# Row chunks behind all products of an input job, and the convolution tile behind the chunks

## The chip, the cores and the metric

The kernel runs on one core of one Trainium2 chip. The metric is the time of one execution on the device in microseconds; the median of several runs is given.

## What is computed

One decoder layer on 256 tokens of width 2048, in float32: a norm, a gated projection, a causal depthwise convolution of 31 taps, a layer norm, an output projection, and an MLP. Six vectors, made from a condition `c`, scale and shift it. Cut to what matters:

```python
mod = silu(c) @ mod_w + mod_b
sh1, sc1, g1, sh2, sc2, g2 = split(mod, 6)
h = rms_norm(x, norm1_g) * (1 + sc1) + sh1
a, gt = split(h @ conv_w_in + conv_b_in, 2)
u = depthwise_conv(a * sigmoid(gt), conv_dw_w) + conv_dw_b   # 31 taps, causal
u = silu(layer_norm(u, conv_ln_g, conv_ln_b))
x = x + (1 + g1) * (u @ conv_w_out + conv_b_out)
h = rms_norm(x, norm2_g) * (1 + sc2) + sh2
x = x + (1 + g2) * (square(relu(h @ mlp_w1)) @ mlp_w2)
```

## The kernel before

Activations lie with channels on the 128 partitions and 256 tokens in the free dimension: 16 tiles of 128 channels. Weights come as blocks of 1 MB through the tag `raw` with seven buffers, in one fixed order that `order` lists and `top_up` issues on SyncE's queue; a block is issued when a buffer comes free. Each weight block is split by `split_w` into a rounded part `hi` (ScalarE, L206) and a rest `lo` (L209, on GpSimd for the input jobs), in halves, so that products in a fast format keep float32's precision.

The work is a list of `jobs`: 16 input jobs, 8 output jobs, then the MLP's. Input jobs 0 to 7 are done in the first stage while the columns of `sc1` and `sh1` arrive. Input jobs 8 to 15 stand in the loop shown below, and `n` is their number. Such a job

- makes the gate's two channel tiles: `mm` issues 64 products (L234 and L235; job 15 uses a merged form, L230 to L232) in four quarters, two outputs by two halves of the contraction, into one of two accumulators of the tag `mm` (one accumulator has two PSUM banks);
- runs up to four **row chunks**. `mod_chunk` (L310) multiplies the condition with one block of `mod_w`; the rows for `g1` and `sc2` make 32 chunks: 4 in each of jobs 8 to 12, 3 in job 13, 9 in job 15. A chunk is four matmuls of 32 columns of the array, eight records in the trace. When 16 chunks are done the sums are copied (L317) and turned into columns (L357);
- evacuates its accumulator (`evac`, L518 on ScalarE and L519 on VectorE) and gates it (`gate`, L750 and L752);
- from job 9 on runs one **convolution tile** on TensorE (`mix`, `pe_conv`, L735): 32 matmuls of 32 columns, 64 records, into an accumulator of the same tag `mm`; ScalarE copies it out (L743). The operand is a widened copy of `u` (`copy_wide`, L712, two buffers). Eight more channel tiles are convolved on VectorE, tap by tap (`advance`, L621 to L630). After the second convolution tile, `find_shift` sums two tiles (L410), and ScalarE copies the negative mean (L670), which VectorE adds (L625, L674).

The layer norm's sums over channels are taken by `stats` in groups of four tiles: ScalarE squares them (L462, one buffer `sq`), and TensorE sums tiles and squares (L680). Group 0 and group 1 stand behind job 14's products, group 2 behind the convolution tile of job 15. Then come two row chunks, the last convolution tile (into the tag `acc`), the last sums and the norm itself.

A scheduler fixes each engine's order when the program is built: of what is ready by its own estimate of times it takes the piece written first (pieces in `urgent()` come earlier). `tc.issue_after(ins)` adds one bound: what stands inside is queued behind `ins` on the same engine. It does not wait for `ins` to finish, and it does not keep other work out from between.

Of the kernel before, what the change touches and what calls it, by code (L numbers as in the profile page):

```python
# [66 lines left out]
def conv_block(ctx: ExitStack, tc: tile.TileContext, x, vec, dwq, c_row, mod_r, mod_c, w_first, w_in, w_out, w1, w2, out):  # L67
# [50 lines left out]
    state = {"used": 0}  # L118
# [103 lines left out]
    def mm(p, c, key, acts_of, ks=range(KT), merged=False):  # L222
        halves = parts[key]
        for k in ks:
            hi, lo = halves[k // HALF]
            m = acts_of[k // 2][:, k % 2, :]
            if merged:
                out_p, begin, end = p[:, c, 0:T], k == 0, k == KT - 1
                w = hi[:, k % HALF, :]
                nc.tensor.matmul(out_p, w, m[:, 0:T], start=begin, stop=False)  # L230
                nc.tensor.matmul(out_p, w, m[:, T : 2 * T], start=False, stop=False)  # L231
                state["mm_end"] = nc.tensor.matmul(out_p, lo[:, k % HALF, :], m[:, 0:T], start=False, stop=end)  # L232
                continue
            nc.tensor.matmul(p[:, c, :], hi[:, k % HALF, :], m, start=(k == 0), stop=(k == KT - 1))  # L234
            state["mm_end"] = nc.tensor.matmul(  # L235
                p[:, c, T : 2 * T], lo[:, k % HALF, :], m[:, 0:T], start=False, stop=(k == KT - 1),
                skip_group_check=True,
            )
# [62 lines left out]
    def mod_chunk(nb, kg):  # L301
        w = take(("mod", nb, kg))
        group = next(g for g in GROUPS if nb in g)
        b = group.index(nb)
        begin, end = b == 0 and kg == 0, b == len(group) - 1 and kg == 3
        if begin:
            mod_finish()
            row_ps.append(ps.tile([P, 512], F32, name="row", bufs=1))
        for k in range(4):
            state["row_end"] = nc.tensor.matmul(  # L310
                row_ps[0][32 * k : 32 * k + 32, :], cz[:, 4 * kg + k, 3 - b : 35 - b], w[:, 4 * k : 4 * k + 4, :],
                start=begin, stop=end,
            )
        if end:
            r = tmp.tile([P, 512], F32, name="rowsb", bufs=1)
            with urgent(), tc.issue_after(state["hi_end"]):
                nc.scalar.activation(r, row_ps.pop(), AF.Copy)  # L317
            pending.append(([4 * nb for nb in group], 4, r))

    def shift_row(at, w):  # L320
        if at == 0:
            row_ps.append(ps.tile([P, 512], F32, name="row", bufs=1))
        for k in range(KT):
            g = k % 4
            nc.tensor.matmul(
                row_ps[0][32 * g : 32 * g + 32, at * P : (at + 1) * P], shz[:, k, :], w[:, k, :],
                start=(k < 4), stop=(k >= KT - 4),
            )

    def fold_shift():  # L330
        n = 2 * UNSCALED
        r = tmp.tile([P, 512], F32, name="rowsb", bufs=1)
        p = ps.tile([P, 512], F32, name="row", bufs=1)
        with urgent():
            nc.scalar.activation(r[:, 0 : n * P], row_ps.pop()[:, 0 : n * P], AF.Copy)
            for j in range(n):
                nc.tensor.matmul(p[:, j : j + 1], r[:, j * P : (j + 1) * P], col("pick", 0, 1), start=True, stop=True)
            nc.scalar.activation(shc, p[:, 0:n], AF.Copy)
# [40 lines left out]
    def mod_col(at, w=None):  # L379
        w = (take(("col", at)) if w is None else w).rearrange("p k n -> p (k n)")  # L380
        which, k = divmod(at, KT)
        acc = modc[:, at : at + 1]
        if which == SH2 and "cond" in state:
            n = HALF * P
            for half, total in zip(state["cond"], (acc, rest2[:, k : k + 1])):
                nc.vector.scalar_tensor_tensor(w[:, 0:n], w[:, 0:n], 1.0, half, op0=ALU.mult, op1=ALU.mult, accum_out=total)
                w = w[:, n:]
            return
        with tc.issue_after(state["e_end"]) if "e_end" in state else ExitStack():
            nc.vector.scalar_tensor_tensor(w, w, 1.0, cb, op0=ALU.mult, op1=ALU.mult, accum_out=acc)  # L390
        if which in amps:
            return nc.vector.scalar_tensor_tensor(
                amps[which][:, k : k + 1], acc, col("modb", at), col("n1g", k), op0=ALU.add, op1=ALU.mult
            )
        elif which != SH2:
            return mod_bias(at, 1, acc)

    def mods(keys):
        for key in keys:
            if key[0] == "mod":  # L400
                mod_chunk(*key[1:])
            else:
                mod_col(key[1])
# [28 lines left out]
    def two():  # L432
        return tmp.tile([P, 2, T], F32, name="two", bufs=6)
# [26 lines left out]
    def squares(src, s=None):  # L460
        s = cp.tile([P, 4, T], F32, name="sq", bufs=1) if s is None else s
        nc.scalar.activation(s, src, AF.Square)  # L462
        return s
# [8 lines left out]
    def by_tokens(job):  # L472
        return job[0] == "down" or job[0] == "up" and job[1:] not in ((0, 0), (0, 1))
# [133 lines left out]
    def cv(k):  # L607
        return cvs[k // 4][:, k % 4, :]
# [67 lines left out]
    def sum_round(pairs, first=False, last=()):  # L676
        for n, tiles in enumerate(zip(*pairs)):
            for m, t in enumerate(tiles):
                g = 2 * n + m
                state["stats_end"] = nc.tensor.matmul(  # L680
                    state["small"][32 * g : 32 * g + 32, 0:T], ones[:, 0:32], t, start=first, stop=m in last,
                )

    def stats(b):
        s = squares(cvs[b])
        for k in range(2):
            sum_round([(cv(4 * b + 2 * m + k), s[:, 2 * m + k, :]) for m in range(2)], b == 0 and k == 0)
# [69 lines left out]
    def mix(ct):  # L757
        pe_conv(ct)
        if ct == SHIFT - 1:
            find_shift()  # L760
# [15 lines left out]
    for n, job in enumerate(jobs):  # L776
# [22 lines left out]
        if job == ("up", 0, 0):  # L799
            mm(p, 0, job + (0,), xa, range(SIDE))  # L800
            for at in range(2 * UNSCALED):
                shift_row(at, shown.pop(("up", 0, at // 2, at % 2)))
            fold_shift()
            mm(p, 0, job + (0,), xa, range(SIDE, KT))
            mm(p, 1, job + (1,), xa)
        elif job in K_OUTER:
            for k2 in range(HALF):
                for c in range(2):
                    mm(p, c, job + (c,), xa if plain else hl, range(2 * k2, 2 * k2 + 2), kind == "out")
        elif kind == "in":  # L810
            rows = [key for key in after[job] if key not in cols_in] if i < KT - 1 else []
            for c in range(2) if i < KT - 1 else (1, 0):
                for ks in (range(HALF), range(HALF, KT)):
                    mm(p, c, job + (c,), hl, ks, i == KT - 1)
                    with tc.issue_after(state["mm_end"].ins):
                        mods(rows[:1])
                    del rows[:1]
        elif by_tokens(job):
            mm_tokens(sums[kind, i // 2], job, u2 if kind == "down" else hl, n == len(jobs) - 1)
        else:  # L820
            for c in range(2):
                mm(p, c, job + (c,), hl, merged=kind == "out")
        mod_finish()
        if kind == "in":
# [11 lines left out]
                for key, w in taken:  # L836
                    mod_col(key[1], w)
            for ct in CONV_AT.get(n, ()):
                with tc.issue_after(state["mm_end"].ins):
                    mix(ct)  # L840
            advance(ADVANCE.get(n, 0))
            if n == KT - 2:
                with tc.issue_after(state["mm_end"].ins):
                    for b in range(2):
                        stats(b)
            if n < KT - 1:
                continue
            sq15 = two()
            with tc.issue_after(state["conv_end"].ins):
                stats(2)  # L850
            rows = list(after[job])
            with tc.issue_after(state["stats_end"].ins):
# [226 lines left out]
```

## Time and profile before

| | us |
|---|---|
| median of 3 runs | 1103.8 |
| lowest and highest | 1103.57, 1103.97 |
| the profiled execution | 1103.93 |
| its span, first to last instruction | 1102.1 |

| engine | busy us | share of the span |
|---|---|---|
| TensorE (PE) | 1085.5 | 98% |
| its weight loads (PEld) | 892.8 | 81% |
| VectorE (DVE) | 746.3 | 68% |
| ScalarE (ACT) | 510.2 | 46% |
| GpSimd (POOL) | 192.7 | 17% |

The span is 1.8 us shorter than the time of the execution. L310 and the like are lines of the kernel. "Busy" counts the time in which an engine has an instruction in work; gaps of TensorE between matmuls of different kinds are not seen in it, since matmuls are pipelined and their ends are modelled. A row of the chain gives start, length and what ran, followed back from the last instruction; "x8" counts records.

### The profile page before, as it was taken

What the parts mean: (1) busy time and instruction counts of PE and PEld (TensorE: products, weight loads), DVE (VectorE), ACT (ScalarE), POOL (GpSimd) and SP (SyncE); (2) the same over time, 40 slices, a digit from 0 to 9 for tenths busy, and PEclk for the clock granted to TensorE, in tenths of its full rate; (3) what the DMA queues carried; (4) which work ended last, traced back from release to release, by engine and by line L of the source; (5) the groups of instructions that cost most, each with busy time, mean ns of one, the idle gap of its engine ahead of it and who ended that gap; (6) DMA issues with size and microseconds to landing.
All of it is one profiled execution on the core that took longest, in us unless ns stands there. A gap on an engine that the chain in (4) does not pass through costs nothing.

```text
span 1102.1 us, 15388 instructions
## 1 busy us (share of the span) xinstructions
PE 1085.5 (98%) x6018; PEld 892.8 (81%) x6018; DVE 746.3 (68%) x1025; ACT 510.2 (46%) x679; POOL 192.7 (17%) x119
## 2 busy tenths in 40 slices
PE   7999999999999999999999999999999999999998
PEld 4887876667599998888888888888888888888887
DVE  5777789989676966678954667545566665565653
ACT  4111296665676587444443444333444333444431
POOL 0000076468679252000000000000000000000000
PEclk9999999999999999999999999999999999999999
DMA  9999999876899966898976889657888877789611
GB/s 385 421 420 420 416 408 356 349 288 264 321 359 419 402 240 232 255 317 304 418 285 218 237 267 319 236 141 290 249 234 245 234 210 210 229 247 244 206 67 39
DMA packets 142316, 314.23 MB, mean 285 GB/s; under 512 B 87586, under 2 KB 105506, under 8 KB 107298
## 3 DMA queue, kind: packets, MB, share of 16 engines
q1 hardware_dynamic: 142096, 313.11, 80.8%
q8 instruction: 47, 0.77, 0.3%
q14 instruction: 27, 0.21, 0.1%
q10 hardware_dynamic: 146, 0.13, 0.0%
HBM read 301.15 MB, written 12.07 MB: 284 GB/s over the span
## 4 chain that ended last, share of the span: by engine, by line
PE 88%; DMA 9%; DVE 2%; ACT 1%; issue 0%; SPq 0%; ACTq 0%
PE mm L258 20%; PE mm L257 20%; PE mm L259 20%; DMA raw<-mod_c 9%; PE mm L234 6%; PE mm L235 3%; PE acc L232 2%; PE acc L231 2%; PE acc L230 2%; PE mm L735 2%; PE row L310 2%; DVE raw L390 1%; PE mm L231 1%; DMA x<-x 1%; PE mm L230 1%; PE mm L232 1%
## 5 line engine op out<-in xcount | busy, mean ns | idle before, releaser
L206 ACT ACTIVATE hi<-raw 128x1024 fp32r<-128x1024 f32 x320 | 335.6, 1058 | 367.9 <-PE mm L259 333.6
L209 DVE TENSOR_TENSOR lo<-raw,hi 128x1024 fp32r<-128x1024 f32 x257 | 313.2, 1223 | 193.5 <-ACT hi L206 191.4
L258 PE MATMUL mm<-lo,u 128*128 128x512 f32 x496 | 193.0, 389 | 0.0
L257 PE MATMUL mm<-hi,u 128*128 128x512 f32 x496 | 193.0, 389 | 0.0
L259 PE MATMUL mm<-hi,u 128*128 128x512 f32 x496 | 192.9, 389 | 0.0
L209 POOL TENSOR_TENSOR lo<-raw,hi 128x1024 fp32r<-128x1024 f32 x63 | 154.3, 2476 | 199.1 <-DMA raw<-w_in 132.2
L259 PE MATMUL mm<-hi,hl 128*128 128x512 f32 x480 | 186.7, 389 | 0.0
L258 PE MATMUL mm<-lo,hl 128*128 128x512 f32 x480 | 186.7, 389 | 0.0
L257 PE MATMUL mm<-hi,hl 128*128 128x512 f32 x480 | 186.7, 389 | 0.0
L390 DVE SCALAR_TENSOR_TENSOR raw<-raw,cond 128x2048 f32<-128x2048 f32 x50 | 118.2, 2366 | 39.8 <-DMA raw<-mod_c 39.6
L259 PEld LDWEIGHTS mm<-hi,u 128*128 128x128 f32 x496 | 93.1, 188 | 19.4
L258 PEld LDWEIGHTS mm<-lo,u 128*128 128x128 f32 x496 | 93.1, 188 | 19.0
L257 PEld LDWEIGHTS mm<-hi,u 128*128 128x128 f32 x496 | 93.1, 188 | 19.0
L257 PEld LDWEIGHTS mm<-hi,hl 128*128 128x128 f32 x480 | 90.1, 188 | 18.8
L259 PEld LDWEIGHTS mm<-hi,hl 128*128 128x128 f32 x480 | 90.1, 188 | 18.7
L258 PEld LDWEIGHTS mm<-lo,hl 128*128 128x128 f32 x480 | 90.1, 188 | 18.7
L627 DVE SCALAR_TENSOR_TENSOR acc<-u,v,acc 128x256 f32<-128x256 f32 x224 | 94.4, 483 | 1.8
L234 PE MATMUL mm<-hl,hi 128*128 128x512 f32 x224 | 81.7, 406 | 0.0
L562 PE MATMUL mm<-two,first 128*128 128x256 f32 x256 | 61.1, 394 | 7.6 <-ACT two L593 7.5
L562 PEld LDWEIGHTS mm<-two,first 128*128 128x128 f32 x256 | 49.9, 197 | 17.5 <-ACT two L593 10.4
L232 PE MATMUL acc<-hl,lo 128*128 128x256 f32 x224 | 63.5, 283 | 0.0
L235 PE MATMUL mm<-hl,lo 128*128 128x256 f32 x224 | 63.4, 283 | 0.0
(183 smaller groups left out, 1278.6 us busy)
## 6 DMA issues: line engine op xcount, KB each, us to landing
raw<-w SPq DMA_DIRECT2D x128, 1024.0 KB, 5.4
raw<-mod_c SPq DMA_DIRECT2D x62, 1024.0 KB, 11.4
raw<-mod_r SPq DMA_DIRECT2D x32, 1024.0 KB, 7.8
raw<-w_in SPq DMA_DIRECT2D x16, 1024.0 KB, 8.0
raw<-w_out SPq DMA_DIRECT2D x16, 1024.0 KB, 7.8
first<-w_first SPq DMA_DIRECT2D x15, 1024.0 KB, 19.8
flat<-two SPq DMA_DIRECT2D x30, 256.0 KB, 2.7
two<-flat SPq DMA_DIRECT2D x120, 64.0 KB, 4.1
```

The source lines that it names most:

```text
L206: state["w_hi"] = nc.scalar.activation(hi, w[:, ks, :], AF.Copy).ins
L209: end = by.tensor_tensor(lo, w[:, ks, :], hi.bitcast(F32), op=ALU.subtract)
L230: nc.tensor.matmul(out_p, w, m[:, 0:T], start=begin, stop=False)
L232: state["mm_end"] = nc.tensor.matmul(out_p, lo[:, k % HALF, :], m[:, 0:T], start=False, stop=end)
L234: nc.tensor.matmul(p[:, c, :], hi[:, k % HALF, :], m, start=(k == 0), stop=(k == KT - 1))
L235: state["mm_end"] = nc.tensor.matmul(p[:, c, T : 2 * T], lo[:, k % HALF, :], m[:, 0:T], start=False, stop=(k == KT - 1), skip_group_check= ...
L257: nc.tensor.matmul(p, p_hi, hi, start=begin, stop=False)
L258: nc.tensor.matmul(p, p_hi, lo, start=False, stop=False)
L259: nc.tensor.matmul(p, p_lo, hi, start=False, stop=end)
L390: nc.vector.scalar_tensor_tensor(w, w, 1.0, cb, op0=ALU.mult, op1=ALU.mult, accum_out=acc)
L562: step = nc.tensor.matmul(held[n][:, c, :], w[:, 2 * n + c, :], h, start=k == 0 and c == 0, stop=k == KT - 1, skip_group_check=True)
L627: nc.vector.scalar_tensor_tensor(out, s, w, acc, op0=ALU.mult, op1=ALU.add)
```

## The change

In the input jobs 8 to 14 the chunks are no longer queued one behind each quarter of the products; all of a job's chunks are queued behind the job's last product. The convolution tile is no longer queued behind the last product but behind the last chunk, where the job has chunks. Group 0 of the norm's sums is queued behind the convolution tile of job 14 and not behind its last product. Group 1 moves from job 14 to job 15: it is queued behind that job's convolution tile, ahead of group 2.

```diff
             for c in range(2) if i < KT - 1 else (1, 0):
                 for ks in (range(HALF), range(HALF, KT)):
                     mm(p, c, job + (c,), hl, ks, i == KT - 1)
-                    with tc.issue_after(state["mm_end"].ins):
-                        mods(rows[:1])
-                    del rows[:1]
+            state["step_end"] = state["mm_end"]
+            with tc.issue_after(state["mm_end"].ins):
+                mods(rows)
+            if rows:
+                state["step_end"] = state["row_end"]
...
             for ct in CONV_AT.get(n, ()):
-                with tc.issue_after(state["mm_end"].ins):
+                with tc.issue_after(state["step_end"].ins):
                     mix(ct)
             advance(ADVANCE.get(n, 0))
             if n == KT - 2:
-                with tc.issue_after(state["mm_end"].ins):
-                    for b in range(2):
-                        stats(b)
+                with tc.issue_after(state["conv_end"].ins):
+                    stats(0)
             if n < KT - 1:
                 continue
             sq15 = two()
             with tc.issue_after(state["conv_end"].ins):
+                stats(1)
                 stats(2)
```

## The prediction

> **What bounds the kernel now.** I read the page first, then the windows of the input jobs, then the chain that ended last through them, then the queues of the other engines there. The page:
>
> ```profile
> PE 1085.5 (98%) x6018; PEld 892.8 (81%) x6018; DVE 746.3 (68%) x1025; ACT 510.2 (46%) x679; POOL 192.7 (17%) x119
> PE 88%; DMA 9%; DVE 2%; ACT 1%; issue 0%; SPq 0%; ACTq 0%
> ```
>
> TensorE is busy 98% of the span and is 88% of the chain. Whether it also works at its best rate is another question, because the chain counts the gaps between kinds of matmul as work. The changed code runs from 138 to 294 us, so the windows there come next (columns: stretch, length, then busy time and count of PE, PEld, DVE, ACT, POOL, then granted clock, DMA share, GB/s):
>
> ```profile
> 169.40:184.40 15.00, 15.00 (x92) 10.20 (x96) 14.78 (x38) 11.27 (x21) 8.81 (x5) 1.00 0.95 343
> 231.00:244.80 13.80, 13.80 (x82) 10.02 (x82) 11.54 (x24) 11.28 (x21) 5.17 (x4) 1.00 0.89 344
> 250.10:261.60 11.50, 11.50 (x68) 9.79 (x64) 10.80 (x23) 3.66 (x4) 11.50 (x6) 1.00 0.93 370
> ```
>
> These are the products of jobs 10, 13 and 14, each from its first to its last product. TensorE never stops and the granted clock is 1.00. Job 14 has no row chunk among its 64 products and takes 11.50 us; job 10 has three and takes 15.00, job 13 has two and takes 13.80. So a chunk alone among products costs 3.50/3 = 1.17 or 2.30/2 = 1.15 us. DVE is busy 14.78 of 15.00 us in job 10: it is nearly a second bound. The chain (start, length, what) shows where the chunks (L310, eight records each) and convolution tiles (L735, 64 records each) stand:
>
> ```profile
> 149.12 0.99 PE row L310 x8
> ...
> 164.89 2.94 PE mm L735 x51
> 168.04 0.67 PE row L310 x5
> ...
> 172.03 0.99 PE row L310 x8
> ...
> 178.97 0.99 PE row L310 x8
> ...
> 197.19 1.00 PE row L310 x8
> ...
> 205.94 0.89 PE row L310 x6
> ...
> 227.09 1.72 PE row L310 x16
> ...
> 232.59 0.99 PE row L310 x8
> ```
>
> Two things are to be seen. First, beside a convolution tile two chunks take 1.72 us, 0.86 each, against 1.15 to 1.17 alone: a block of 32-column work inside the products costs 0.30 us over its work (1.16 - 0.86). Second, no chunk of jobs 8 to 12 runs before its own job's products are over, although the code lets the first go after a quarter of them. Job 8's begin at 149.12, behind its last product; job 9's run at 168.04 in the convolution tile and from 172.03 to 178.97, three of them, among job 10's products. Were the transfers late? SyncE's timeline, and the line on its loads from 120 to 240 us:
>
> ```profile
> 150.60 7.64 SPq L187 DMA_DIRECT2D raw<-mod_r  x4
> ```
> ```profile
> DMA to landing us min/median/max: 4.7/7.9/16.4
> ```
>
> Job 9's four transfers are issued from 150.60 to 158.24 and land a median 7.9 us later, about 158.5 to 166.1 (an estimate from these two rows). The chunks run 9 to 13 us after that. TensorE takes its queue in order, and that order was fixed ahead by the scheduler: it had held the chunks to be late, some 3.5 us apart ((178.97 - 172.03)/2).
>
> **The change part by part.** No matmul, transfer or byte is added or removed; the order on TensorE changes, and with it when buffers and results come free.
>
> *Row chunks behind all four quarters.* They were behind them already, so this bound alone moves nothing in jobs 8 to 12: 0 us.
>
> *Convolution tile behind the last chunk.* Here the order decides. If the scheduler still holds job 9's last chunk to be late, the tile of job 9 can't go at 164.89; job 10's products are free to go first, and the tile follows the chunk of 178.97, so each tile slips by nearly a job. Now count the blocks among the products. Jobs 9 and 10: before, three chunks alone and one beside the tile; after, three alone and the last beside it: 0. Job 11: two of four stood beside the tile (the first at 205.94), after one: +1 block. Job 12: two at 227.09 and a third stood beside the tile, only 232.59 alone; after, one or two more alone: +1. Job 13: 0 to +1. The shift's sums (L410), which shared blocks with job 10's chunks: 0 to +1. I take +3 blocks at 0.30 = +0.9 us, bounds +0.3 and +1.5.
>
> *The cover that goes.* Until now each tile stood between two jobs' products, and the evacuation of a job ran under it (timelines of ScalarE and VectorE):
>
> ```profile
> 184.44 0.60 ACT L518 ACTIVATE two<-mm 128x512 f32<-128x512 f32 x1 [3.56 <-PE mm L235]
> 185.80 0.47 ACT L750 ACTIVATE two<-mm,v 128x256 f32<-128x256 f32 x1 [0.77 <-DVE mm L519]
> 188.92 0.47 ACT L743 ACTIVATE cv<-mm,v 128x256 f32<-128x256 f32 x1 [2.64 <-PE mm L735]
> ```
> ```profile
> 186.85 0.48 DVE L752 SCALAR_TENSOR_TENSOR u<-mm,v,two 128x256 f32<-128x256 f32 x1
> ```
>
> From the end of job 10's products to a free accumulator are 2.9 us (184.44 to 187.33). There are two accumulators. With the tile gone from between, the next job's products go into the other one, and the job after that waits for the late tile's copy, 0.47 us and a hand-over on each side, at most 0.7 us where the tile ends just ahead of a job's end. No row shows this wait; its bounds are 0 and 0.7 in each of five jobs. I take 0.2 each, +1.0 us, nearer to nought since the tile usually ends some us ahead.
>
> *Late shift.* The second tile moves from job 10's last product at 184.40 to behind 197.19, so it ends near 202, and the shift that DVE adds comes after that (the same timelines):
>
> ```profile
> 196.76 0.39 ACT L670 ACTIVATE shift<-small 128x256 f32<-128x256 f32 x1
> ```
> ```profile
> 197.81 0.87 DVE L625 SCALAR_TENSOR_TENSOR acc<-u,v,small 128x256 f32<-128x256 f32 x2
> ```
>
> L625 would be held to about 203.5, 5.7 us. What hides it is the even taps of the same two tiles, 15 each, which need no shift. I take 0; without that cover DVE, which has 2.26 us of idle time in the window from 231.00, runs up to 3.4 us late.
>
> *The norm's sums.* They move from between to behind the tiles; the chain has them now so:
>
> ```profile
> 265.29 1.28 PE small L680 x20
> ...
> 271.19 0.99 PE small L680 x12
> ...
> 279.44 3.59 PE mm L735 x64
> 283.03 0.86 PE small L680 x16
> ```
>
> and on ScalarE, in the timeline:
>
> ```profile
> 272.29 1.06 ACT L462 ACTIVATE sq<-cv 128x1024 f32<-128x1024 f32 x1 [1.47 <-PE small L680]
> ...
> 281.34 3.14 ACT L712 ACTIVATE wide<-u 32x284 f32<-32x284 f32 x7 [0.56 <-DVE u L752]
> ```
>
> Groups one and two cost 1.28 + 0.99 = 2.27 us now and 2 x 0.86 = 1.72 in two closed blocks; and the block inside the last products goes, 0.30. That saves 0.85. But the squares have one buffer. ACT squares group three at 272.29, 0.11 us after the second group's sums left it. When those stand behind the last tile, this squaring falls between them and the third group, with the later chunks and the last tile queued behind: 0.11 + 1.06 + some 0.1 back = 1.3 us of idle TensorE, up to 1.8 if the copies of 281.34 go first. Net +0.4 us, bounds 0 and +0.9.
>
> *Sum.* +0.9 + 1.0 + 0.4 = +2.3 us on the profiled execution's 1103.93 us, 1106.2; that run stands 0.13 above the median of 1103.8, so 1106.1. From 294 us on TensorE is busy or waits on the norm, so nothing gives it back.
>
> *The skill on a block's price.* The Trainium skill, TensorEngine Tiling (Array Packing), Key Properties, says that a change of tiling mode drains the array; the 0.30 us here bear that out. Its page TensorE: Matmul & The Clock Gate, Single matmul latency, gives 166 ns as the fixed part when warm; two drains would be 0.33 us, an estimate, and three blocks +1.0 in place of +0.9.
>
> *The skill against bunching.* The products' weight loads, in the answer on their line (shortest, median and longest ns):
>
> ```profile
> L234 PEld LDWEIGHTS mm<-hl,hi x190: 186/188/190, 138.0 to 244.2; 128*128 128x128 f32 x190
> ```
>
> A job's 64 products with 64 such loads take 11.50 us, 0.18 each, less than one load: they overlap. The Trainium skill, TensorE: Matmul & The Clock Gate, The mechanism, lets a load overlap matmuls in flight only in another row group; by that the loads, and not the switches, would be the cost, and bunching would gain nothing. The trace disagrees, so this weighs nothing.
>
> **The rivals.** *A, the rows do stand together:* the scheduler keeps job n+1's products behind tile n, for instance because accumulators are handed out in the code's order. Then of 14 chunks alone (four of job 8, three each of 9 and 10, two of 11, one each of 12 and 13) one block is left, 13 x 0.30 = -3.9 us, with the sums' +0.4: -3.5, 1100.3 (0.25 to 0.35 a block: 1099.7 to 1101.0). For it: the transfers have landed by then, by the estimate above job 9's last at 166.1 when it would be wanted at about 167. Against it: the code orders nothing between a tile and the next job. *S, an accumulator is missing at a job's end:* a tile slips so far that both are held, and the products wait the whole 2.9 us. It decides where the last chunk comes within 3.6 us of the next job's end: the chunk of 178.97 and 3.59 us of tile end at about 183.5, the job at 184.9. One job so: 1109.0; three: 1114.8. *N, the order stays nearly as it is* and only the sums move: 1104.2.
>
> **How the numbers follow.** Forecast 0.50, own range 1104.1 to 1108.5 (blocks and sums at their bounds, the waits from 0 to two thirds of 3.5); A 0.31; S 0.13; N 0.06. A measurement of this kernel tells 0.2%, 2.2 us. Faster: A, 0.32 with an odd chance. Slower than 1106.0: somewhat over half of the forecast, 0.27, and S 0.13: 0.40. Within: the rest, 0.28. The range goes from A's lower end, 1099.8, to one job of S, 1109.5.
>
> **What would show it.** Right: L735 records of job 9 near 180 and not 165; chunks still apart among the products; L462 once behind 282 with TensorE idle over 1 us ahead of the last L680. Rival A: all four L310 of a job in one run ahead of L735, products of a job in 11.5 us. S: idle time ahead of L234, ended by ACT L743 or DVE L752. Wrong altogether: a DVE that is late for L519, or transfers that land behind their chunk.

## The result, and the profile after

The kernel with the change takes 1109.72 us (median of 6 runs, 1109.24 to 1110.05) against 1103.71 us before (6 runs, 1103.57 to 1103.97): a ratio of 1.0054, 95% interval 1.0041 to 1.0067. That is 6.0 us slower, where the forecast had +2.3 us and the range ended at 1109.5 us. The profiled execution took 1109.74 us, its span is 1107.9 us.

The page of the changed kernel, the rows that answer to the first ones shown of before:

```profile
PE 1083.7 (98%) x6018; PEld 892.9 (81%) x6018; DVE 740.6 (67%) x1025; ACT 509.6 (46%) x679; POOL 194.6 (18%) x119
PE 81%; DMA 10%; DVE 5%; ACT 3%; issue 1%; DVEq 0%; SPq 0%
L234 PE MATMUL mm<-hl,hi 128*128 128x512 f32 x224 | 82.2, 408 | 5.7 <-DVE u L752 5.7
```

TensorE is still 98% busy, but it has fallen from 88% to 81% of the chain of waits, and VectorE has risen from 2% to 5%. The third row says where: the products wait 5.7 us for the gate, L752. That wait was not there before. Next the chain that ended last, for the input jobs from 9 on (start, length, what):

```profile
171.73 21.93 DVE acc L627 x56
193.66 0.78 DVE rest L627 x2
194.43 0.61 DVE mm L519
...
196.07 0.48 DVE u L752
196.68 0.77 PE mm L234
...
210.78 3.57 PE row L310 x32
214.35 2.16 PE mm L735 x40
...
230.42 3.57 PE row L310 x32
233.99 3.45 PE mm L735 x64
```

Two things are to be seen. The chunks of a job now stand in one run (x32 is four chunks) directly ahead of the job's tile: this is rival A's order, not the forecast's. And from 171.73 to 196.68 us the chain is on VectorE: 56 taps of the convolution, and only behind them job 10's evacuation L519. TensorE's timeline at that place, the end of job 10:

```profile
183.24 3.64 PE L310 MATMUL row<-raw,cz 128*32 128x512 f32 x32
186.70 3.63 PE L735 MATMUL mm<-wide,diag 128*32 128x256 f32 x64
190.26 0.70 PE L410 MATMUL small<-cv,ones 128*128 128x256 f32 x2
196.68 0.77 PE L234 MATMUL mm<-hl,hi 128*128 128x512 f32 x1 [5.72 <-DVE u L752]
```

Job 10's products end 1.1 us earlier than before (183.3 against 184.40 us), the chunks and the tile follow without a gap, and then TensorE stands still for 5.72 us: job 11's products need the accumulator in which job 10's result still lies. VectorE's timeline says why it lies there, first of the changed kernel, then of the kernel before:

```profile
171.64 22.02 DVE L627 SCALAR_TENSOR_TENSOR acc<-u,v,acc 128x256 f32<-128x256 f32 x56
193.57 0.86 DVE L627 SCALAR_TENSOR_TENSOR rest<-u,v,acc 128x256 f32<-128x256 f32 x2
194.36 0.69 DVE L519 TENSOR_TENSOR mm<-mm,two 128x512 f32<-128x512 f32 x1
196.07 0.47 DVE L752 SCALAR_TENSOR_TENSOR u<-mm,v,two 128x256 f32<-128x256 f32 x1
207.49 0.88 DVE L625 SCALAR_TENSOR_TENSOR acc<-u,v,small 128x256 f32<-128x256 f32 x2 [10.50 <-ACT shift L670]
```
```profile
171.56 12.62 DVE L627 SCALAR_TENSOR_TENSOR acc<-u,v,acc 128x256 f32<-128x256 f32 x32
185.06 0.70 DVE L519 TENSOR_TENSOR mm<-mm,two 128x512 f32<-128x512 f32 x1 [0.89 <-ACT two L518]
```

Before, 32 taps stood ahead of L519, and L519 waited 0.89 us for its operand. Now 56 taps and two more pieces stand ahead, and no wait is shown: the operand lay ready. It was ready at 183.95 us, by ScalarE's row:

```profile
183.35 0.60 ACT L518 ACTIVATE two<-mm 128x512 f32<-128x512 f32 x1 [1.88 <-PE mm L235]
```

So L519 started 10.4 us after it could have. The windows around the stall (columns as in the prediction) give its price:

```profile
190.90:196.70 5.80, 0.08 (x2) 0.05 (x1) 5.80 (x16) 1.62 (x3) 0.13 (x1) 0.85 1.01 422
196.70:202.60 5.90, 5.90 (x20) 5.04 (x21) 0.29 (x1) 5.78 (x13) 4.59 (x2) 0.57 0.54 189
202.60:210.70 8.10, 8.10 (x48) 6.95 (x46) 3.21 (x9) 4.78 (x10) 4.68 (x2) 1.00 0.28 116
```

In the first TensorE is idle and VectorE busy all the time. In the second TensorE is busy again, but at a granted clock of 0.57: 20 records take 5.90 us, 0.295 each, against 8.10/48 = 0.169 in the third. The 20 would have taken 3.4 us, so some 2.5 us are lost beside the 5.7 us of standing (an estimate, since the trace can lack some records of matmuls).

The end of the input jobs, where the norm's sums now stand behind the tile of job 15 (282.68 us, against 279.37 before), on TensorE and on ScalarE:

```profile
287.02 0.60 PE L680 MATMUL small<-cv,ones 128*32 128x256 f32 x4
288.91 0.41 PE L680 MATMUL small<-sq,ones 128*32 128x256 f32 x2 [1.29 <-ACT sq L462]
```
```profile
284.64 3.14 ACT L712 ACTIVATE wide<-u 32x284 f32<-32x284 f32 x7 [0.55 <-DVE u L752]
287.81 1.06 ACT L462 ACTIVATE sq<-cv 128x1024 f32<-128x1024 f32 x1
```

The squaring of group 2 stands behind the seven copies L712, and TensorE waits 1.29 us for it. The last tile then starts at 292.25 us; before it did at 286.17 us.

### The profile page after: what moved, and what is told of

It reads as the page before. It is cut to its first block, busy times and chain, and to the rows that moved or that the text cites. A ratio compares the mean times of both kernels' runs of the same rounds, so it can differ in the third digit from the quotient of the medians.

```text
span 1107.9 us, 15389 instructions
## 1 busy us (share of the span) xinstructions
PE 1083.7 (98%) x6018; PEld 892.9 (81%) x6018; DVE 740.6 (67%) x1025; ACT 509.6 (46%) x679; POOL 194.6 (18%) x119
## 4 chain that ended last, share of the span: by engine, by line
PE 81%; DMA 10%; DVE 5%; ACT 3%; issue 1%; DVEq 0%; SPq 0%
PE mm L258 20%; PE mm L257 20%; PE mm L259 20%; DMA raw<-mod_c 7%; PE mm L234 4%; DVE acc L627 3%; PE acc L232 2%; PE acc L231 2%; PE acc L230 2%; PE mm L235 2%; DMA first<-w_first 2%; ACT wide L712 1%; PE mm L735 1%; PE row L310 1%; DMA raw<-w_in 1%; DVE raw L390 1%
## 5 line engine op out<-in xcount | busy, mean ns | idle before, releaser
L390 DVE SCALAR_TENSOR_TENSOR raw<-raw,cond 128x2048 f32<-128x2048 f32 x50 | 116.3, 2328 | 40.3 <-DMA raw<-mod_c 40.3
L234 PE MATMUL mm<-hl,hi 128*128 128x512 f32 x224 | 82.2, 408 | 5.7 <-DVE u L752 5.7
```

## The experiments

The working theory from this profile, called theory 1 or T1 below: the bunched chunks bring about 3 us, the sums cost about 1 us, and VectorE's queue, in which taps stand ahead of job 10's evacuation, costs about 8 us. The measured times in one place:

| kernel | median us (range, runs) | ratio to before, 95% interval |
|---|---|---|
| the change | 1109.72 (1109.24 to 1110.05, 6) | 1.0054 [1.0041, 1.0067] |
| rows_only | 1108.2 (1108.17 to 1109.14, 5) | 1.0042 [1.0027, 1.0056] |
| sums_only | 1104.99 (1104.54 to 1108.32, 10) | 1.0016 [1.0007, 1.0025] |
| taps_at_10 | 1101.8 (1101.64 to 1102.18, 10) | 0.9982 [0.9973, 0.9991] |
| taps_behind_gate | 1105.85 (1105.64 to 1107.72, 10) | 1.002 [1.0011, 1.0029] |
| touch_first | 1112.61 (1111.72 to 1112.97, 4) | 1.0076 [1.0059, 1.0093] |
| taps10_rows_only | 1100.53 (1100.4 to 1100.7, 6) | 0.997 [0.9958, 0.9981] |
| rows_bound_only | 1102.85 (1102.77 to 1103.32, 10) | 0.9992 [0.9983, 1.0002] |
| taps10_other_squares | 1099.95 (1099.72 to 1100.16, 5) | 0.9964 [0.9951, 0.9977] |
| tile_bound_only | 1113.85 (1113.58 to 1114.45, 4) | 1.0091 [1.0076, 1.0107] |
| job8_together | 1105.55 (1104.95 to 1106.47, 10) | 1.0017 [1.0008, 1.0026] |
| job8_taps9 | 1099.28 (1099.22 to 1099.54, 5) | 0.9961 [0.9948, 0.9973] |

**The two parts of the change apart.** rows_only is the change without the sums' move:

```diff
-                with tc.issue_after(state["conv_end"].ins):
-                    stats(0)
+                with tc.issue_after(state["mm_end"].ins):
+                    for b in range(2):
+                        stats(b)
...
-                stats(1)
```

> The change without its second part: chunks and tiles as in the changed kernel, the norm's sums as before. Theory T1 (the loss is made in job 11: VectorE has some 56 taps queued ahead of job 10's evacuation, so TensorE waits 5.7 us for the accumulator and then runs about 2.5 us slower at a lower granted clock; bunching itself gains about 3.2; the sums cost about 1.2): 1109.7 - 1.2 = 1108.5 us, with the idle time ahead of L234 still near 5.7 us. Rival T3 (the sums' move is the larger part of the loss): 1105 or less.

sums_only is the kernel before with the same lines the other way round: the sums' move alone.

> Only the norm's sums are moved; chunks and tiles as before. T1: 1103.7 + 1.2 = 1104.9 us, with 1.0 to 1.8 us of idle TensorE ahead of the third group's sums of squares. The prediction's term was +0.4 (0 to 0.9): 1104.1. T3: 1107 or more.

rows_only took 1108.2 us and has the wait for L752 of 5.7 us, but no wait ahead of the sums. sums_only took 1104.99 us, +1.2 against the 1103.77 us of before beside it, and has a wait of 1.3 us for the squares. Its ten runs spread from 1104.54 to 1108.32 us, so its difference alone is weak; two kernels further down give the same size. So most of the loss sits in the chunks and tiles, not in the sums.

**Is it the taps?** In taps_at_10 the change stays as it is, and the taps that are written behind job 10's gate are also queued behind it:

```diff
-        nc.vector.scalar_tensor_tensor(
+        state["u_end"] = nc.vector.scalar_tensor_tensor(
             u[i][:, PAD : PAD + T], t2[:, 0, :], ...
...
-            advance(ADVANCE.get(n, 0))
+            with tc.issue_after(state["u_end"].ins) if n == 10 else ExitStack():
+                advance(ADVANCE.get(n, 0))
```

> The changed kernel, and the taps written behind job 10's gate are queued behind that gate on VectorE; TensorE's order stays as it is. T1: job 10's gate ends about 3 us after its products and not 13, the wait of 5.7 us and the slow products go, 1109.7 - 8.2 = 1101.5 us. Rival T2 (VectorE is held by the late shift, the wait of 10.5 us ahead of L625, and the order of taps is only a sign of it): the shift is as late as before, TensorE still waits, 1107 or more.

It took 1101.8 us: 7.9 us less than the change, and 1.9 less than before. VectorE's and TensorE's rows there, the second pair from the windows:

```profile
184.01 0.70 DVE L519 TENSOR_TENSOR mm<-mm,two 128x512 f32<-128x512 f32 x1 [0.34 <-ACT two L518]
185.25 0.48 DVE L752 SCALAR_TENSOR_TENSOR u<-mm,v,two 128x256 f32<-128x256 f32 x1 [0.54 <-ACT two L750]
```
```profile
190.60:194.40 3.80, 3.80 (x22) 3.30 (x21) 3.76 (x11) 3.71 (x9) 2.39 (x2) 1.00 1.03 427
194.40:202.70 8.30, 8.30 (x51) 7.04 (x53) 6.48 (x15) 6.08 (x12) 3.55 (x2) 1.00 0.87 365
```

L519 again waits for its operand and not the other way round, job 11 starts at once, and the clock stays at 1.00. The edit binds nothing but VectorE's queue, so that queue's order is the 7.9 us. The two parts of it can be read: job 11's products up to the second pair of the shift's sums (L410) take 3.54 us here (190.65 to 194.19) and 5.76 us in the change (196.68 to 202.44), so the low clock cost 2.2 us and not 2.5, and 5.7 + 2.2 = 7.9.

**The same bound at every job.** taps_behind_gate drops the condition `if n == 10`.

> The same for the taps of every input job. T1: no wait of TensorE for L752 in any job, 1101 to 1102 us, unless VectorE now runs out of taps in some job and ends them too late for the norm; then up to 1104. T2: 1107 or more.

It missed: 1105.85 us. No wait of TensorE for L752 is left, but one of 4.05 us for the squares has come (its row stands in the last section). VectorE's rows and ScalarE's say why:

```profile
273.01 6.25 DVE L627 SCALAR_TENSOR_TENSOR acc<-u,v,acc 128x256 f32<-128x256 f32 x12
279.17 0.48 DVE L752 SCALAR_TENSOR_TENSOR u<-mm,v,two 128x256 f32<-128x256 f32 x1
```
```profile
279.68 3.13 ACT L712 ACTIVATE wide<-u 32x284 f32<-32x284 f32 x7 [3.31 <-DVE u L752]
```

Twelve of the taps that were held back now stand ahead of job 15's gate, although ScalarE had its operand ready at 276.4 us. ScalarE's seven copies wait 3.31 us for that gate, and the squares stand behind the copies. It is the mechanism of the change again, one engine further on.

**With and without the sums.** taps10_rows_only joins rows_only and the bound at job 10.

> Chunks and tiles as in the changed kernel, the norm's sums as before, and the taps behind job 10's gate. T1: 1101.8 - 1.2 = 1100.6 us. If the sums' move costs nothing beside the other two: 1101.8.

1100.53 us, 3.2 less than before: this is what bunching the chunks is worth. (The bound on the taps is in it too and was not run by itself; but the kernel before has no wait of TensorE for L752 that it could remove.) taps_at_10 has the sums' move on top and takes 1.3 us more, about as sums_only did. taps10_other_squares is taps_at_10 with group 2's squares in two buffers of the tag `two` in place of the one `sq`:

```diff
-        s = squares(cvs[b])
+        if b == 2:
+            pair_sq = [squares(cvs[b][:, 2 * m : 2 * m + 2, :], two()) for m in range(2)]
+        else:
+            s = squares(cvs[b])
+            pair_sq = [s[:, 0:2, :], s[:, 2:4, :]]
...
```

> The changed kernel with the taps behind job 10's gate, and the third group's squares in two other buffers, so that they need not wait for the second group's sums. If the single buffer of the squares is what the sums' move costs: the idle time of 1.3 us ahead of the last L680 goes, 1101.8 - 1.3 = 1100.5 us. If the sums' length is the cost: 1101.8.

1099.95 us, 1.85 less than taps_at_10, and the wait ahead of the sums is gone. The move of the sums, without that wait, gains 0.6 us (1100.53 to 1099.95).

**The two bounds apart.** rows_bound_only has the chunks behind all four quarters, but the tile still behind the last product; tile_bound_only has the tile behind the last chunk, but the chunks still one behind each quarter. In both the sums stand as before.

> Only the chunks' bound is moved behind all products; the tile stays bound to the last product and the sums stay. By the prediction's step that the chunks stood behind the products already: 1103.7 us, within 0.3. If this bound alone bunches the chunks: 1100 to 1101, or 1108 with the wait in job 11.

> The kernel before with the tile's bound alone: the convolution tile is queued behind the job's last chunk; the chunks stay bound one behind each quarter, the sums stay as before. Theory 1 (the tile, which now comes later, holds the next job's products behind it by the order of the accumulators, and this makes the taps go ahead of job 10's evacuation): the stall of 8.2 us is there without the chunks' bound, and the chunks, one behind each quarter, stand apart inside their own job's products: 16 alone (four of job 8, three each of jobs 10 to 13) against 14 before, +0.6 us: 1103.8 + 8.2 + 0.6 = 1112.6 us (1111 to 1113.5), TensorE's wait for the gate L752 near 191 us again. Theory 2 (the stall comes from all chunks standing behind the job): no such wait, 1104.4 us.

The first took 1102.85 us: no difference beyond 0.2%, but 0.84 below the 1103.69 us of before beside it, with no overlap of their runs, where "within 0.3" was expected. One block is gone in its trace, some 0.3 of this: job 13's first chunk, among the products at 242.43 us before, stands at 243.51 us directly ahead of the tile (244.40). The second took 1113.85 us, 0.35 above the upper end of what was expected. It has both things that theory 1 gave it, the wait and the chunks apart (TensorE's waits, then its timeline in job 12):

```profile
PE mm L234 <- DVE u L752: 5.9, 1, 5.9
```
```profile
225.60 1.06 PE L310 MATMUL row<-raw,cz 128*32 128x512 f32 x8
229.62 1.07 PE L310 MATMUL row<-raw,cz 128*32 128x512 f32 x8
233.59 1.06 PE L310 MATMUL row<-raw,cz 128*32 128x512 f32 x8
237.62 1.06 PE L310 MATMUL row<-raw,cz 128*32 128x512 f32 x8
```

The tile's bound alone brings the stall. The chunks' bound alone is worth 0.8 us, but beside the tile's bound it is worth 5.7 us (1113.85 to 1108.2 in rows_only): bound to quarters only, 16 chunks stand alone among products, and in rows_only four. From its first product to its tile job 10 takes 15.88 us here (171.82 to 187.70) and 14.95 us in rows_only (171.88 to 186.83), so three chunks alone cost 0.93 us, 0.31 each. Twelve make 3.7 of the 5.7 us; where the other 2.0 us come from stays open.

**Why the products did not go ahead of the tile.** In touch_first, the next job's accumulator is allocated, and VectorE writes one column of it, ahead of the tile in the code. The write adds an instruction that the computation does not need.

```diff
...
+            if n < KT - 1:
+                state["next_p"] = ps.tile([P, 2, 2 * T], F32, name="mm", bufs=2)
+                nc.vector.memset(state["next_p"][:, 0, 0:1], 0.0)
```

> The changed kernel, but VectorE writes one column of the next job's accumulator ahead of the convolution tile in the code (seven small writes that the products overwrite). This tests the step that the prediction got wrong, that the next job's products are free to go ahead of the tile. Theory U (an accumulator goes to whoever uses the tag first in the code, so the tile kept the products behind it): now the products go first, chunks stand apart again, the tile comes behind the last chunk in the middle of the next job, and the prediction's own sum applies: 1106.1 us (1104.1 to 1108.5). Rival V (something else, the weights or the squares, held the products): TensorE's order as in the changed kernel, 1109.7.

TensorE's timeline near the end of job 9's chunks, now among job 10's products:

```profile
176.53 1.07 PE L310 MATMUL row<-raw,cz 128*32 128x512 f32 x8
179.48 1.07 PE L310 MATMUL row<-raw,cz 128*32 128x512 f32 x8
180.36 3.64 PE L735 MATMUL mm<-wide,diag 128*32 128x256 f32 x64
```

This is the order that was forecast for the change: chunks apart, and the tile of job 9 near 180 us. So it is the accumulators' order of use, written in the code, that keeps job n+1's products behind tile n. The time, 1112.61 us, missed the 1106.1 that went with this order: the squares come late for the sums,

```profile
PE small L680 <- ACT sq L462: 5.4, 1, 5.4
```

and the matmuls after them run slowly. ScalarE's seven copies, which stand ahead of the squares (from 285.00 us), wait 4.67 us for job 15's gate; VectorE does that gate at 284.49 us, behind a piece of 3.41 us (L390, a column of `mod`). What put it there is not shown. The wait is 4.1 us longer than the change's 1.29, and the slow stretch behind it costs 2.9 us (last section). Without both, 1105.6 us would be left, an estimate, near the 1106.1. So the run shows the order; for the forecast's sum it is only a hint, since its terms were not measured apart.

**The mechanism at another place.** Job 8's four chunks still stand apart in all versions. In job8_together (from taps10_other_squares) job 9's first products are queued behind job 8's last chunk (`HELD` is 8); job8_taps9 also holds back the taps of job 9:

```diff
-                    mm(p, c, job + (c,), hl, ks, i == KT - 1)
+                    with tc.issue_after(state["step_end"].ins) if n == HELD + 1 and c == 0 and ks == range(HALF) else ExitStack():
+                        mm(p, c, job + (c,), hl, ks, i == KT - 1)
```
```diff
-            with tc.issue_after(state["u_end"].ins) if n == 10 else ExitStack():
+            with tc.issue_after(state["u_end"].ins) if n in (9, 10) else ExitStack():
```

> Taps at job 10 bound behind its gate and group 2's squares in other buffers, as in the version of 1099.95 us, and job 9's first products queued behind job 8's last chunk, so that job 8's four chunks stand in one run. Three blocks of 0.30 us go: 1099.1 us if TensorE's blocks alone decide. Theory 1 (VectorE's queue decides): in this build job 9's evacuation L519 stands behind 17 more instructions of VectorE than before, 17 x 0.43 = 7.3 us; its gate ends near 175.6 us and TensorE wants that accumulator near 171.0 us, so it idles about 4.6 us there and runs at a low clock after it, about 2.3 us more: 1099.1 + 6.9 = 1106.0 us (1104.5 to 1107.5).

> The same as the kernel with job 8's chunks in one run, and the taps of job 9 are queued behind that job's gate too. Theory 1: job 9's evacuation comes in time again, no wait for the gate near 171 us, three blocks of 0.30 us less than 1099.95 us: 1099.1 us (1098.7 to 1099.6). If a block inside the products costs nothing of its own and only the stall counted: 1099.95 us.

Both came out as theory 1 had them: 1105.55 and 1099.28 us. VectorE in the first, TensorE where it stops, and its windows from there:

```profile
172.93 0.70 DVE L519 TENSOR_TENSOR mm<-mm,two 128x512 f32<-128x512 f32 x1
...
174.70 0.49 DVE L756 SCALAR_TENSOR_TENSOR u<-mm,v,two 128x256 f32<-128x256 f32 x1
```
```profile
175.33 0.77 PE L234 MATMUL mm<-hl,hi 128*128 128x512 f32 x1 [4.70 <-DVE u L756]
```
```profile
175.30:181.30 6.00, 5.97 (x19) 5.14 (x20) 5.68 (x13) 5.87 (x14) 4.57 (x2) 0.54 1.02 431
181.30:189.20 7.90, 7.90 (x50) 6.78 (x52) 2.14 (x5) 4.11 (x7) 4.59 (x2) 1.00 0.66 276
```

(L756 is the gate in these kernels, four lines further down.) A better order on TensorE made the scheduler put job 9's evacuation behind more of VectorE's work, and the stall appeared one job earlier than in the change, with the same low clock behind it; one bound on VectorE took it away but for 0.31 us, which TensorE still waits for job 9's gate. With it the kernel takes 1099.28 us, 0.4% less than before. It is the best version found.

## Why the prediction was wrong, step by step

That the kernel got slower, as forecast, is luck: none of the three terms of the +2.3 us came as it was worked out. Three other terms, each from a difference of runs, make up the 6.0 us: bunched chunks -3.2 (taps10_rows_only to before), the sums +1.3 (taps_at_10 to taps10_rows_only), VectorE's queue +7.9 (the change to taps_at_10).

*"Job 10's products are free to go first, and the tile follows the chunk".* This step failed, and with it the forecast's order. They are not free: tile and products share the tag `mm`, and the accumulators go round in the order in which the code first uses them. touch_first shows it. The text had this reason, as rival A's, and set against it that "the code orders nothing between a tile and the next job"; two buffers of one tag are such an order. So the chunks stood in one run, and the tile of job 9 at 168.18 us and not near 180. What would have told: the front of the document says that the tile uses an accumulator of the same tag.

*The blocks.* Forecast +0.9 us, with three blocks more. In the order that came, ten blocks went, -3.2 us, 0.32 each: of the 14 chunks alone before, only job 8's four still stand alone. Rival A counted 13, because it let job 8's four stand together too. In job8_taps9 three more went for 0.67 us, 0.22 each, with the 0.31 us of waiting in it. The price of a block was right, its count was that of the other order.

*"They were behind them already, so this bound alone moves nothing".* Nearly right (rows_bound_only, 1102.85 us, 0.8 less than before), but the two bounds were weighed one at a time. Beside the tile's bound the chunks' bound decides between 1113.85 and 1108.2 us.

*The cover that goes.* Forecast +1.0 us, for products that wait a little for the late tile's copy. No wait for that copy, L743, came. What came was a wait for the gate. Jobs and tiles take the two accumulators in turn, so a job gets the one in which the job before it lay, and not "the other one": its products wait for that job's gate, as the row of 196.68 us shows. This is the second step that failed: the cover was priced with the evacuation's 2.9 us from the trace of before, as if it would stay that long. From the end of job 10's products at 183.3 us to a free accumulator at 196.5 us it is 13.2 us in the changed kernel. That the chunks and the tile, 7.1 us, still stood between as cover was not enough. This is the missing term, +7.9 us, which no case of the prediction held: A was worked out as if VectorE's order would stay the same when TensorE's changes. The text named the sign, "a DVE that is late for L519", and had read that VectorE is busy 14.78 of 15.00 us in job 10, "nearly a second bound", but gave it no price.

*Late shift.* Taken at 0, held up 5.7 us. L625 started at 207.49 us after 10.50 us of waiting, and it cost TensorE nothing: that wait began at 197.0 us, when TensorE's stop was over, and no later wait of TensorE in the input jobs is for VectorE. Most of it came with the stop: in taps_at_10 the second pair of L410 is done 8 us earlier, and L625 waits 1.54 us.

*The sums.* Forecast +0.4 us, bounds 0 and +0.9; it was +1.3. The cause of the wait was right, one buffer for the squares, for with two others it went. That its size was met (1.3 us, measured 1.29) is in part luck: the copies of L712 did go ahead of the squaring, the case that was given 1.8 us, and four records of tile sums, the row of 287.02, ran meanwhile. What was mis-sized is the rest. The saving of 0.85 us was 0.58 (1100.53 to 1099.95), and with the wait the sums of tiles and squares no longer run side by side: taps10_other_squares got back 1.85 us, the 1.29 and 0.56 more.

*Rivals.* A gave the order and 1100.3 us; taps10_rows_only with the order of A and without the sums' move took 1100.53, and taps_at_10, with it, 1101.8. That is 1.5 us above A's figure: 0.7 from the blocks that stayed and 0.9 from the sums, less 0.1 because before took 1103.7 and not 1103.8. S had the right kind of place, idle time ahead of L234 ended by DVE L752, and too small a price, 2.9 us and no low clock, and another cause, a tile that slips. Why the scheduler put 24 more taps ahead of L519 is not shown. That it took job 10's products, now behind chunks and tile, for later than they are, and filled the time, would fit, and job8_together behaves the same way; its own estimates are not in any trace. The ends of the range, 1099.8 and 1109.5, are not quite the 1099.7 and 1109.0 that the sums of A and S give.

## What to carry to other kernels

A new bound on one engine changes the order on the others: before it is given a price, look which results the next-busiest engine must hand back, and how much work could be put ahead of them. Two uses of one tag are an order between them, even where the code writes none. Two bounds in one change are to be weighed together: here one was worth 0.8 us alone and 5.7 us beside the other.

## What the runs showed of the hardware

The price of a stop of TensorE is more than its length. After 5.72 us of standing the clock was 0.57 in the next 5.9 us, which cost 2.2 us; after 4.70 us in job8_together it was 0.54 in the next 6.0 us. A stop of 4.05 us was enough too, by two rows of taps_behind_gate and one of the change:

```profile
283.95 0.41 PE L680 MATMUL small<-sq,ones 128*32 128x256 f32 x2 [4.05 <-ACT sq L462]
285.15 3.27 PE L310 MATMUL row<-raw,cz 128*32 128x512 f32 x14
```
```profile
289.80 1.89 PE L310 MATMUL row<-raw,cz 128*32 128x512 f32 x14
```

The same 14 records take 3.27 us behind a stop of 4.05 us, and 1.89 us behind the one of 1.29 us. From the first sums behind the stop to the start of the last tile it is 3.33 us in taps_at_10 (280.81 to 284.14, behind 1.29 us), 5.02 us in taps_behind_gate (283.95 to 288.97, behind 4.05 us) and 6.22 us in touch_first (289.26 to 295.48, behind 5.41 us). So stops of 4.05 to 5.72 us cost 1.7 to 2.9 us on top of their length, and not in step with it. The Trainium skill, TensorE: Matmul & The Clock Gate, What's actually happening, says that TensorE falls to half its clock after an idle window of about 3.4 us and comes back after a busy one. The trace agrees with the threshold, since 4.05 us is above it and 1.29 us below, and with the rate: 0.50 in touch_first from 289.26 to 294.50 us, and 0.54 to 0.57 in the windows above, which take in the return to full clock.
